# A fourth buffer for the raw weight tiles of a two-layer decoder, paid for with half the descriptor scratch of the software DMAs

## The chip, the cores and the metric

One core of a Trainium2 chip runs the whole program. The metric is the device time of one execution in microseconds (us). Before the change it is 982.41 us, the median of three runs (982.23 to 983.89 us).

## What is computed

The reference is a decoder trunk of two layers over 256 tokens of width 1024, in float32. Each layer is a half-step SwiGLU feed-forward network (FFN), a token-mixing block with three head groups, and a second half-step FFN, each followed by a layer norm of the scaled residual:

```python
def swiglu(x, wg, wu, wd):
    return (jax.nn.silu(x @ wg) * (x @ wu)) @ wd

for l in range(DEPTH):
    x = layer_norm(ALPHA * x + 0.5 * swiglu(x, ffn_wg[l, 0], ffn_wu[l, 0], ffn_wd[l, 0]), ln_g[l, 0], ln_b[l, 0])
    m = token_mix(x, w_in[l], w_out[l], ...)
    x = layer_norm(ALPHA * x + m, ln_g[l, 1], ln_b[l, 1])
    x = layer_norm(ALPHA * x + 0.5 * swiglu(x, ffn_wg[l, 1], ffn_wu[l, 1], ffn_wd[l, 1]), ln_g[l, 2], ln_b[l, 2])
```

`wg` and `wu` are 1024 x 2816, `wd` is 2816 x 1024, `w_in` is 1024 x 2344 and `w_out` is 1024 x 1024, so nearly all of the work is weights times activations, and every weight is read from memory once.

## The kernel before

The 256 tokens are two row tiles of 128 (t = 0 and 1). A float32 product is made of three passes of a faster format: both operands are split into a high part and a rest, and `mm3` (lines 262 to 264) issues high times high, high times rest and rest times high into one PSUM bank.

**How a weight reaches TensorE.** Weights come in "halves", tiles of 128 x 1024 floats (512 KB; 128 x 592 for one part of `w_in`). SyncE (SP) issues the load of a half into a tile `raw`. ScalarE (ACT) copies `raw` to `wh`, the high part (line 229 in `split_half`, line 217 in `split_tile`). VectorE (DVE) subtracts, `wl` = `raw` - `wh` (lines 230 and 218), and only then is the `raw` tile free for another load. `raw` has three buffers, `wh` and `wl` have eight each. Two halves are a unit, and `split_weights` makes units one to three ahead of their use. `PLAN`, a string of tokens, sets the order of the units in an FFN.

**Seven products.** For some pairs of weight chunks `seven` replaces eight block products by seven, over sums and differences of weight blocks that DVE builds (line 147). Its loads go to the tiles `fa`, `fb` and `fc`, and those of its function `f4` to two `raw` tiles (line 171, issued at line 143). Those two stay taken from their load until the product called "2", the last of a group, has had them split (line 218). The seven products are issued at line 415 into two PSUM banks. After product "3" DVE adds the bank to a copy (line 465), and product "2" overwrites that bank, so it waits for that add. Product "4", on the other bank, lies between.

**What follows.** Line 478 (ACT) and line 479 (DVE) gate the result into a tile `cc`, line 490 transposes it on TensorE, lines 267 and 268 split the transposed tile, and `down` multiplies by `wd`. The last three `down` units run for t = 0 and then for t = 1, and `layer_norm` (lines 349 to 360, one step of it on GpSimd at line 355) of t = 0 has the `down` work of t = 1 to hide behind. `make_xT` then transposes the normalised rows (line 290) for the next stage. In the mixing block ACT and DVE do, between the same weight splits, the gates (lines 584 to 631), keys and queries and the softmaxes.

**Order.** Inside an FFN the order of TensorE's instructions is pinned. On the other engines, and on TensorE elsewhere, a scheduler sets the order at build time from its own estimate of when buffers and results come free; each engine and each queue then runs its list strictly in order. A wait of ACT or DVE at the head of its list holds all that is behind it, and SP's loads stand in one list too.

**Software DMAs.** GpSimd issues 18 loads (layer norm parameters at line 337, small mixing weights of the second layer at line 535). The descriptors of such loads are written to a scratch area of every SBUF partition, whose size is `dynamic_dma_scratch_size`; a `raw` buffer takes 4096 bytes of a partition.

Of the kernel before, what the change touches and what calls it, by code (L numbers as in the profile page):

```python
# [18 lines left out]
F32 = mybir.dt.float32  # L19
# [38 lines left out]
def build(ctx, tc, d):  # L58
    nc = tc.nc
# [3 lines left out]
    wp = ctx.enter_context(tc.tile_pool(name="wp", bufs=1))  # L63
# [65 lines left out]
    def halves(src, w):  # L129
        units.append(lambda: [split_half(a, w) for a in src])  # L130

    def gate_up(l, f, c, q):
        return [d["wgu"][l, f, c, 2 * q + h] for h in range(2)]

    def seven(l, f, c):


        b11, b12, b21, b22 = [], [], [], []

        def load(to, src, pool, name, tags, bufs):  # L140
            for a, tag in zip(src, tags):
                to.append(pool.tile([128, 1024], F32, name=name, tag=tag, bufs=bufs))
                last_dma[0] = nc.sync.dma_start(out=to[-1], in_=a)

        def less(a, b, to):
            for x, y, z in zip(a, b, to):
                DVE.tensor_sub(out=z, in0=x, in1=y)  # L147

        def parts(ts):
            return [split_tile(x, 1024) for x in ts]  # L150

        def f1():
            load(b11, gate_up(l, f, c, 0), mix, "fa", ("qs0", "qs1"), 1)
            return parts(b11)

        def f5():
            load(b12, gate_up(l, f, c + 1, 0), wp, "fb", ("fb0", "fb1"), 1)
            less(b12, b11, b11)
            return parts(b11)

        def f6():
            load(b22, gate_up(l, f, c + 1, 1), mix, "fc", ("pT", "pT"), 3)
            less(b22, b11, b11)
            return parts(b11)

        def f7():
            less(b22, b12, b12)
            return parts(b12)

        def f4():  # L170
            load(b21, gate_up(l, f, c, 1), wp, "raw", ("raw", "raw"), 3)
            less(b21, b11, b11)
            return parts(b11)

        return {"1": f1, "5": f5, "6": f6, "7": f7, "3": lambda: parts(b22), "4": f4, "2": lambda: parts(b21)}

    for l in range(L):
# [34 lines left out]
    def split_tiles():  # L212
        return (wp.tile([128, 1024], F32R, name="wh", bufs=8), wp.tile([128, 1024], F32R, name="wl", bufs=8))

    def split_tile(raw, w):
        wh, wl = split_tiles()
        ACT.activation(out=wh[:, :w], in_=raw[:, :w], func=AF.Copy)  # L217
        DVE.tensor_sub(out=wl[:, :w], in0=raw[:, :w], in1=wh[:, :w].bitcast(F32))  # L218
        return wh, wl

    def split_half(src, w, parts=1, between=None):
        raw = wp.tile([128, 1024], F32, name="raw", bufs=3)
        wh, wl = split_tiles()
        for i in range(parts):
            s = slice(i * w // parts, (i + 1) * w // parts)
            last_dma[0] = nc.sync.dma_start(out=raw[:, s], in_=src[:, s])
            if between:
                between[i]()
            ACT.activation(out=wh[:, s], in_=raw[:, s], func=AF.Copy)  # L229
            DVE.tensor_sub(out=wl[:, s], in0=raw[:, s], in1=wh[:, s].bitcast(F32))  # L230
        return wh, wl
# [738 lines left out]
    def ffn(l, i, sums, after):  # L970

        f = Ffn(l, i, sums)
        if (l, i) == (0, 0):
            warm_up()
            load_x(0, 0)
            make_xT(0, (0,), sums)
            with tc.issue_after(last_pe[0].ins):
                warm_up()
            first = split_half(gate_up(0, 0, 0, 0)[0], 1024, 2, (lambda: load_x(0, 1), lambda: load_x(1, 0)))
            with tc.issue_after(last_pe[0].ins):  # L980
                make_xT(0, (1,), sums)
            load_x(1, 1)
            made.append([first, split_half(gate_up(0, 0, 0, 0)[1], 1024)])
            f.glu(0, 0, 0)
            with tc.issue_after(x1_after[0].ins):
                make_xT(1, sums=sums)
            f.glu(1, 0, 0)
            f.glu(0, 0, 1)
            f.glu(1, 0, 1)
            f.glu(0, 1, 0)  # L990
        else:
            f.glu(0, 0, 0)
            f.glu(0, 0, 1)
            f.glu(0, 1, 0)
            f.glu(1, 0, 0)
            f.glu(1, 0, 1)
# [118 lines left out]
```

## Time and profile before

| | |
|---|---|
| Median of 3 runs | 982.41 us |
| Profiled execution, its own time | 982.67 us |
| Its span, first to last instruction | 980.9 us |
| TensorE (PE) busy | 959.1 us, 98% of the span |
| DVE busy | 843.2 us, 86% |
| ACT busy | 583.1 us, 59% |
| GpSimd (POOL) busy | 34.8 us, 4% |
| Granted TensorE clock, mean | 0.997 of full speed |
| Read from memory | 176.91 MB, 181 GB/s over the span |
| Loads on the hardware queue | 171.23 MB, 52.8% of 16 DMA engines |
| Loads on the software queue | 6.75 MB, 2.3% |

The profiled execution is 0.26 us above the median. Its time outside the span is 982.67 - 980.9 = 1.8 us. The busy share of PE is a union over overlapping matmuls whose ends are modelled, so idle time of PE is time in which nothing at all was in flight there.

### The profile page before, as it was taken

How to read it: one execution, taken by the hardware profiler on the slowest of the kernel's cores; microseconds unless marked ns; L12 is line 12 of the kernel's file. 1: busy time of each engine (PE TensorE's matmuls, PEld its weight loads, DVE VectorE, ACT ScalarE, POOL GpSimd, SP SyncE). 2: the span in 40 equal slices, each digit the busy share in tenths (PEclk: the TensorE clock that was granted, in tenths of full speed). 3: DMA queues.
4: the chain of work that ended last, by engine and by line, in shares of the span. 5: the costliest groups of instructions: out<-in, count | busy, mean ns of one | idle time of the engine just before them, and what ended most of it. 6: DMA issues, size and time to landing. Idle time of an engine off the chain costs nothing. (4 is left out here: it accounts for less than half of the span.)

```text
span 980.9 us, 12843 instructions
## 1 busy us (share of the span) xinstructions
PE 959.1 (98%) x4611; PEld 780.5 (80%) x4611; DVE 843.2 (86%) x1247; ACT 583.1 (59%) x884; POOL 34.8 (4%) x50
## 2 busy tenths in 40 slices
PE   8999999999999999999999999999999999999996
PEld 5887888777778888888788888877787788888885
DVE  6798997887868988998899799978888699889986
ACT  6565664575764656565556666654667456556651
POOL 0000000020001000000000000001000010000000
PEclk9999999999999999999999999999999999999998
DMA  8765666564454645647673736466534364646251
GB/s 290 270 213 173 213 203 224 179 200 138 149 169 134 219 145 198 208 135 268 204 227 119 256 129 216 148 218 196 177 114 141 129 216 150 209 155 236 90 184 49
DMA packets 51872, 178.80 MB, mean 182 GB/s; under 512 B 6624, under 2 KB 7648, under 8 KB 51552
## 3 DMA queue, kind: packets, MB, share of 16 engines
q1 hardware_dynamic: 49968, 171.23, 52.8%
q0 software_dynamic: 1840, 6.75, 2.3%
q8 instruction: 36, 0.59, 0.2%
q14 instruction: 28, 0.23, 0.1%
HBM read 176.91 MB, written 1.05 MB: 181 GB/s over the span
## 5 line engine op out<-in xcount | busy, mean ns | idle before, releaser
L230 DVE TENSOR_TENSOR wl<-raw,wh 128x1024 fp32r<-128x1024 f32 (+2 forms) x225 | 267.7, 1202 | 60.5 <-ACT wh L229 59.8
L229 ACT ACTIVATE wh<-raw 128x1024 fp32r<-128x1024 f32 (+2 forms) x225 | 231.9, 1039 | 142.4 <-DMA raw<-in_wd 35.9
L217 ACT ACTIVATE wh<-fa 128x1024 fp32r<-128x1024 f32 x96 | 101.3, 1060 | 93.4 <-DVE fa L147 61.2
L262 PE MATMUL acc<-wh,hi 128*128 128x512 f32 x352 | 138.6, 394 | 0.0
L263 PE MATMUL acc<-wl,hi 128*128 128x512 f32 x352 | 137.2, 390 | 0.8 <-DVE wl L230 0.8
L264 PE MATMUL acc<-wh,lo 128*128 128x512 f32 x352 | 137.3, 390 | 0.0
L218 DVE TENSOR_TENSOR wl<-fa,wh 128x1024 fp32r<-128x1024 f32 x96 | 116.0, 1218 | 9.8 <-ACT wh L217 8.9
L263 PE MATMUL g<-wl,xh 128*128 128x512 f32 (+1 forms) x224 | 85.6, 382 | 1.6 <-DVE wl L230 1.6
L264 PE MATMUL g<-wh,xl 128*128 128x512 f32 (+1 forms) x224 | 86.3, 385 | 0.0
L262 PE MATMUL g<-wh,xh 128*128 128x512 f32 (+1 forms) x224 | 85.1, 381 | 0.0
L263 PEld LDWEIGHTS acc<-wl,hi 128*128 128x128 f32 x352 | 66.2, 188 | 14.5 <-DVE wl L230 1.1
L264 PEld LDWEIGHTS acc<-wh,lo 128*128 128x128 f32 x352 | 66.1, 188 | 13.9
L262 PEld LDWEIGHTS acc<-wh,hi 128*128 128x128 f32 x352 | 66.1, 188 | 13.8 <-ACT wh L229 0.4
L263 PE MATMUL acc<-wl,xh 128*128 128x512 f32 x128 | 51.5, 403 | 1.7 <-DVE wl L230 1.7
L262 PE MATMUL acc<-wh,xh 128*128 128x512 f32 x128 | 51.3, 402 | 1.1 <-ACT wh L229 1.1
L264 PE MATMUL acc<-wh,xl 128*128 128x512 f32 x128 | 50.5, 394 | 0.0
L262 PE MATMUL tr<-wh,xh 128*128 128x512 f32 x128 | 50.2, 392 | 0.0
L263 PEld LDWEIGHTS g<-wl,xh 128*128 128x128 f32 x224 | 42.1, 188 | 10.1 <-DVE wl L230 2.9
L264 PE MATMUL tr<-wh,xl 128*128 128x512 f32 x128 | 49.9, 390 | 0.0
L263 PE MATMUL tr<-wl,xh 128*128 128x512 f32 x128 | 49.8, 389 | 0.0
L262 PEld LDWEIGHTS g<-wh,xh 128*128 128x128 f32 x224 | 42.1, 188 | 8.2 <-issue 0.8
L264 PEld LDWEIGHTS g<-wh,xl 128*128 128x128 f32 x224 | 42.1, 188 | 6.9
(287 smaller groups left out, 1936.0 us busy)
## 6 DMA issues: line engine op xcount, KB each, us to landing
raw<-in_wgu SPq DMA_DIRECT2D x103, 512.0 KB, 4.1
raw<-in_wd SPq DMA_DIRECT2D x88, 512.0 KB, 4.5
raw<-in_win SPq DMA_DIRECT2D x32, 512.0 KB, 4.0
fa<-in_wgu SPq DMA_DIRECT2D x24, 512.0 KB, 4.1
fb<-in_wgu SPq DMA_DIRECT2D x24, 512.0 KB, 4.6
fc<-in_wgu SPq DMA_DIRECT2D x24, 512.0 KB, 4.8
raw<-in_wout SPq DMA_DIRECT2D x16, 512.0 KB, 3.8
lnp_ln_g<-in_ln_g POOLq DMA_DIRECT2D x5, 512.0 KB, 4.5
```

The source lines that it names most:

```text
L217: ACT.activation(out=wh[:, :w], in_=raw[:, :w], func=AF.Copy)
L218: DVE.tensor_sub(out=wl[:, :w], in0=raw[:, :w], in1=wh[:, :w].bitcast(F32))
L229: ACT.activation(out=wh[:, s], in_=raw[:, s], func=AF.Copy)
L230: DVE.tensor_sub(out=wl[:, s], in0=raw[:, s], in1=wh[:, s].bitcast(F32))
L262: pe(PE.matmul(ps, xh, wh, start=start, stop=False))
L263: pe(PE.matmul(ps, xh, wl, start=False, stop=False))
L264: pe(PE.matmul(ps, xl, wh, start=False, stop=stop))
```

## The change

The `raw` tiles get a fourth buffer, at both places that allocate them, and the scratch of the software DMAs goes from 8192 to 4096 bytes per partition.

```diff
         def f4():
-            load(b21, gate_up(l, f, c, 1), wp, "raw", ("raw", "raw"), 3)
+            load(b21, gate_up(l, f, c, 1), wp, "raw", ("raw", "raw"), 4)
...
     def split_half(src, w, parts=1, between=None):
-        raw = wp.tile([128, 1024], F32, name="raw", bufs=3)
+        raw = wp.tile([128, 1024], F32, name="raw", bufs=4)
...
-    nc = bacc.Bacc("TRN2", target_bir_lowering=False, num_devices=1, dynamic_dma_scratch_size=8192)
+    nc = bacc.Bacc("TRN2", target_bir_lowering=False, num_devices=1, dynamic_dma_scratch_size=4096)
```

No instruction is added or taken away. The scheduler, which knows of the fourth buffer, orders some instructions anew. POOL's list is the same, PE's differs at some 30 places outside the pinned stretches, and ACT's, DVE's and SP's lists differ at many.

SP, in the second FFN, around the two `raw` loads of `f4` (line 143); `in_wd` are weights of `down`:

```order
 L226 DMA raw<-in_wd 128x1024 x4
-L143 DMA raw<-in_wgu 128x1024
+L143 DMA raw<-in_wgu 128x1024 x2
 L143 DMA fb<-in_wgu 128x1024 x2
-L143 DMA raw<-in_wgu 128x1024
-L226 DMA raw<-in_wd 128x1024
+L226 DMA raw<-in_wd 128x1024 x2
 L143 DMA fc<-in_wgu 128x1024 x2
```

The two loads of `f4` stand together, and two loads of `down` weights instead of one stand ahead of the next `fc`.

DVE, in the last group of seven products of the same FFN, around the add after product "3" (line 465):

```order
 L479 SCALAR_TENSOR_TENSOR cc<-cc 128x256
 L218 TENSOR_TENSOR wl<-raw,wh 128x1024 x2
-L230 TENSOR_TENSOR wl<-raw,wh 128x1024
+L230 TENSOR_TENSOR wl<-raw,wh 128x1024 x2
 L465 TENSOR_TENSOR cc<-g_4000,cc 128x512
 L230 TENSOR_TENSOR wl<-raw,wh 128x1024
```

One more weight split stands ahead of the add. The same difference is in the last group of each of the four FFNs.

DVE, at the end of the same FFN, ahead of the layer norm of t = 0 (line 349):

```order
 L230 TENSOR_TENSOR wl<-raw,wh 128x1024
 L479 SCALAR_TENSOR_TENSOR cc<-cc 128x256
-L230 TENSOR_TENSOR wl<-raw,wh 128x1024 x2
+L230 TENSOR_TENSOR wl<-raw,wh 128x1024 x3
 L268 TENSOR_TENSOR lo<-tr_4357,hi 128x512
 L268 TENSOR_TENSOR lo<-tr_4366,hi 128x512
-L230 TENSOR_TENSOR wl<-raw,wh 128x1024 x3
+L230 TENSOR_TENSOR wl<-raw,wh 128x1024
 L349 SCALAR_TENSOR_TENSOR x_98<-x_98,acc_3457 128x512
```

One split moves ahead of the two rests of the transposed tile (line 268), and one leaves the stretch between them and the layer norm.

## Rows read from the trace of the kernel before

**Rows 1.** Stretches: busy us and count of PE, PEld, DVE, ACT, POOL; clock, DMA share, GB/s

```profile
0.00:25.00 25.00, 21.23 (x89) 14.40 (x90) 17.07 (x23) 15.34 (x22) 1.60 (x10) 1.00 0.84 291
...
75.00:250.00 175.00, 170.19 (x828) 138.68 (x827) 152.36 (x250) 104.95 (x177) 9.64 (x12) 1.00 0.58 188
...
475.00:500.00 25.00, 23.46 (x108) 19.06 (x107) 22.44 (x31) 13.58 (x17) 1.86 (x2) 1.00 0.65 202
500.00:650.00 150.00, 150.00 (x681) 123.75 (x680) 136.68 (x149) 93.28 (x118) 1.63 (x3) 1.00 0.54 181
650.00:725.00 75.00, 71.08 (x378) 58.66 (x377) 60.98 (x127) 41.15 (x80) 6.70 (x7) 1.00 0.53 174
...
950.00:980.90 30.90, 23.09 (x106) 18.85 (x104) 19.67 (x29) 5.52 (x7) 1.85 (x2) 0.91 0.25 87
```

**Rows 2.** Waits of PE: waiter <- releaser: us in total, times, longest us

```profile
PE acc L263 <- DVE wl L230: 2.5, 4, 1.0
PE tr L290 <- DVE x L360: 2.4, 2, 1.5
PE g L263 <- DVE wl L230: 1.6, 2, 0.8
PE acc L107 <- DVE zw L110: 1.2, 1, 1.2
PE tr L490 <- DVE cc L479: 1.2, 1, 1.2
PE acc L262 <- ACT wh L229: 1.1, 2, 0.7
PE tr L290 <- DMA x<-in_x: 1.0, 2, 0.7
PE tr L290 <- ACT c L584: 0.9, 1, 0.9
PE g L415 <- DVE cc L465: 0.8, 1, 0.8
PE tr L665 <- PE acc L281: 0.7, 2, 0.4
PE tr L290 <- DVE ksl L268: 0.5, 1, 0.5
```

**Rows 3.** Timeline of 478 to 490 us, end of the second FFN, all engines

```profile
479.77 4.04 SPq L226 DMA_DIRECT2D raw<-in_wgu  x3
...
481.13 1.06 ACT L229 ACTIVATE wh<-raw 128x1024 fp32r<-128x1024 f32 x1 [0.81 <-DMA raw<-in_wgu]
...
482.23 1.23 DVE L230 TENSOR_TENSOR wl<-raw,wh 128x1024 fp32r<-128x1024 f32 x1 [0.64 <-ACT wh L229]
483.37 0.68 DVE L349 SCALAR_TENSOR_TENSOR x<-x,acc 128x512 f32<-128x512 f32 x1
...
488.65 0.63 PE L290 MATMUL tr<-ident,x 128*128 128x128 f32 x4 [1.54 <-DVE x L360]
```

**Rows 4.** Instructions on tile raw: who waits on ACT's copy; landing of its loads

```profile
  ACT wh L229: 81.5, 67
...
DMA to landing us min/median/max: 2.7/4.2/8.1
```

**Rows 5.** Timeline of 459 to 468 us, last group of seven, second FFN

```profile
463.09 0.69 DVE L465 TENSOR_TENSOR cc<-g,cc 128x512 f32<-128x512 f32 x1 [1.06 <-PE g L415]
...
464.44 1.06 ACT L229 ACTIVATE wh<-raw 128x1024 fp32r<-128x1024 f32 x1 [4.40 <-DMA raw<-in_wd]
...
465.61 0.39 PE L415 MATMUL g<-wh,xh 128*128 128x512 f32 x1
```

**Rows 6.** Costliest groups: PE's first pass of `down`; busy us, mean ns of one

```profile
L262 PE MATMUL acc<-wh,hi 128*128 128x512 f32 x352 | 138.6, 394 | 0.0
```

**Rows 7.** GpSimd: its step of the layer norm, and its slowest kind of load

```profile
667.54 0.93 POOL L355 TENSOR_TENSOR ve<-ve,mhalf 128x1 f32<-128x1 f32 x1 [22.29 <-DVE ve L354]
...
lnp_ln_b<-in_ln_b POOLq DMA_DIRECT2D x5, 512.0 KB, 5.2
```

## The prediction

> **What bounds the kernel now.** I read the stretches first, because a busy share over the whole span hides where the idle time lies. PE is busy 150.00 of 150 us between 500 and 650 us: in the middle of an FFN it never stops, and nothing that comes earlier there can help [rows 1]. Its idle time lies in few places. It is 25.00 - 21.23 = 3.8 us in the first stretch (first loads), 4.8 us from 75 to 250, 1.5 us from 475 to 500, 3.9 us from 650 to 725 and 7.8 us at the end (the last layer norm and the store). The first and the last do not depend on a buffer that is reused, so what any change of the weight supply can win is in the middle: 4.8 + 1.5 + 3.9 = 10.2 us.
>
> The second view, who PE waited for, says what those 10.2 us are [rows 2]. The waits for `zw` and for `x` are the start, and so are one wait of 1.0 us for a rest `wl` and 0.4 us for a `wh`: 1.2 + 1.0 + 1.0 + 0.4 accounts for 3.6 of the first stretch's 3.8 us. The other waits are 1.5 (`wl` for `acc`), 0.7 (`wh`), 2.4 (layer norm, line 360), 1.6 (`wl` for `g`), 1.2 (line 490), 0.9 (line 584), 0.8 (line 465), 0.7 (line 665) and 0.5 us (`ksl`): 10.3 us.
>
> The third view, the timeline around one of them, shows why a layer norm is late [rows 3]. TensorE stood 1.54 us until 488.65. The norm of t = 0 began at 483.37, when DVE was done with a weight split that began at 482.23. That split had waited for ACT, and ACT had waited 0.81 us for a load to land; the next three `raw` loads left SP over 4.04 us, spread out because each needs a tile that DVE has freed. I followed the stops at 85, 181, 188, 227, 656, 680 and 707 us in the same way, and each led to a `raw` load that landed late: into a split that PE itself needs, or into a split that stood ahead of what PE needs on ACT or DVE.
>
> **What the fourth buffer does.** A load now waits for the split of the tile four before it, not three. A split takes DVE 1.23 us and ACT 1.06 us and a load takes 4.2 us to land (2.7 to 8.1) [rows 3, 4], so a tile is in use some 6.5 us, and three tiles give one half per 6.5 / 3 = 2.2 us, four one per 1.6 us. Where the supply is short, each load leaves one spacing, 1.6 to 2.2 us, earlier. No single stop is longer than 1.54 us, the one for line 360 [rows 2]. In the groups of seven the effect is larger: `f4` holds two tiles until product "2", which leaves the rest of the stream one tile of three now, and two of four after.
>
> The stops that lead to a late load, and go: 1.5 + 0.7 + 2.4 + 1.2 + 0.9 + 0.8 + 0.5 = 8.0 us in ten waits [rows 2]. Two kinds stay. The 1.6 us for `wl` into `g` stand behind DVE's own work of the gates: DVE had no idle time there. The 0.7 us at line 665 are PE after PE. A stop costs a little more than its idle time, because the last matmul before it is counted with its whole 394 ns [rows 6] although in the stream a matmul takes 150.00 / 681 = 0.22 us [rows 1]. That is an estimate of 0.17 us for each, 1.7 us for ten. Sum: 9.7 us.
>
> **What the change may take.** (a) Moved rows. The piece of DVE's order at line 465 puts a second split ahead of the add for which product "2" waits, at four places. The add ran at 463.09 and product "2" started at 465.61, so 465.61 - 463.09 - 0.69 = 1.8 us are to spare, and one split takes 1.23. Now that split's `raw` load landed just before 464.44, ACT having waited 4.40 us for it [rows 5]. If it stayed as late, the add would end at 464.44 + 1.06 + 1.23 + 0.69 = 467.4, 1.8 us after product "2" wants to start. I take it to be early, since its load no longer waits for a tile that `f4` holds. (b) At the layer norm of t = 0 the order has one split fewer ahead, which adds to the gain of rows 3; the two rests at line 268 get one more ahead. (c) In the mixing block some softmax and gate rows change places. The trace of before has no row for their new places. Bounds: below, nothing, or the 1.6 us of the two gate waits gained as well; above, as many new stops as there are old ones, 9.7 us, which undoes the sum. I take three new stops of the mean size of the ten, 3 x 0.8 = 2.4 us, since most of DVE's list is as it was. (d) The scratch. GpSimd issues few loads, far apart: it had waited 22.29 us in front of its step of the layer norm [rows 7]. So I take 0 for it; its upper end is the fourth rival.
>
> Sum: 9.7 - 2.4 = 7.3 us. The profiled execution is 982.67 us, 0.26 above the median, so the forecast is 982.41 - 7.3 = **975.1 us**. Its own range runs from three stops fewer gone to no new stop: 972.5 to 978.5.
>
> **Rivals.** *Loads only share the engines.* With three tiles in flight the DMA engines are already 0.65 busy at 202 GB/s around the stop of 488 us, and the first stretch, where all loads are free to go, reached no more than 291 GB/s at 0.84 [rows 1]. By that ceiling a half of 512 KB takes 1.8 us, and four tiles would give one per 1.8 us instead of 1.6. The trace speaks for some of it (landing times spread up to 8.1 us), and against all of it, since the share in the stretches with stops is 0.53 to 0.65. Half of the 9.7 us would go and the same share of new stops would come, 4.9 - 1.2 = 3.7: 978.7 us. The Trainium skill (DMA: Bandwidth & Descriptors, Issuing engines are not separate DMA queues) says that transfers issued at the same time run on the same 16 engines and interleave, which is this rival; its section Bandwidth puts what memory gives one core at about 358 GB/s, by which a half would take an estimated 1.46 us and this rival would be weak.
>
> *The wait moves.* The splits come earlier, but DVE, busy 136.68 of 150 us in the middle of an FFN [rows 1], or a `wh` buffer that TensorE still reads, ends last at the same places. For it: `wh` is not given a ninth buffer. Against it: of what waits on the `raw` tiles, 81.5 us are ACT's high parts waiting at 67 places [rows 4], and I found loads, not `wh`, at all stops that I count. The time would be within 0.2% of now, about 981.5.
>
> *The added split is late (slower).* The one mechanism is (a): on DVE, in the last group of each FFN, the split ahead of line 465. It decides if its load lands less than 1.8 us earlier than it does now (see (a)). If it lands no earlier at all, product "2" stops by 1.8 us at four places, 7.2 us, and with the layer norms behind it held as now (nothing gained), 982.4 + 7.2 = 989.6 us. Against it: at 464.44 the load had waited for a tile, which it now finds free.
>
> *The half scratch is too small (slower).* If descriptors of a load had to wait for the load before it to land, 5.2 us [rows 7], the next layer norm step on GpSimd could stand behind it. At the four norms with loads ahead of them in the list that would be up to 4 x 5.2 = 20.8 us, less the 7.3 gained: 996 us. The 22.29 us of slack speak against it [rows 7]. The Trainium skill (SBUF — State Buffer, SBUF size: 192, 224, or 256?) has 16 KiB set aside for this scratch as the normal case, four times what is left here; no run here shows the fill.
>
> **How the numbers follow.** Forecast 0.58, shared engines 0.20, the wait moves 0.11, added split 0.07, scratch 0.02, and 0.02 for more than the forecast's own range. A measurement of this kernel can tell some 0.2%, 2 us, from no change. Faster by more than that: 0.58 + 0.20 + 0.02 = 0.80. Within: 0.11. Slower: 0.09. The range leaves out at most 2 in 10: down to 9.7 + 1.6 = 11.3 us gained, 971.1, and up to the moved wait at 981.5.
>
> **What would show it.** Right: the waits of PE for lines 360, 479, 465 and 584 and for `acc`'s weights leave the list or fall under 0.3 us; PE is busy about 25.0 of 25 us around the second FFN's end; ACT's 81.5 us before its high parts from `raw` fall by a third or more. Shared engines: the median landing rises from 4.2 towards 5.6 us and the stops are halved. Added split: waits for line 465 four times. Scratch: POOL's step at line 355 waits for something other than DVE. Wrong altogether: PE's idle time between 25 and 950 us stays near 10 us.

## The result and the profile after

The changed kernel takes 978.29 us (median of 6 runs, 977.75 to 978.65), the kernel before 983.25 beside it (6 runs, 982.23 to 987.17): ratio 0.9938, 95% interval [0.9914, 0.9962]. That is 5.0 us faster by the medians; 7.3 were forecast, and 978.29 lies inside the range. The interval of the ratio means a gain of 3.7 to 8.5 us, so this measurement alone does not tell 5.0 from 7.3. The profiled executions are 982.67 us before (span 980.9) and 978.65 after (span 976.9).

The same stretches as in [rows 1], in the kernel after:

```profile
0.00:25.00 25.00, 20.94 (x87) 14.39 (x88) 17.16 (x23) 16.39 (x24) 1.60 (x10) 1.00 0.83 284
75.00:250.00 175.00, 172.91 (x845) 141.67 (x844) 154.24 (x254) 107.89 (x180) 9.59 (x12) 1.00 0.58 189
475.00:500.00 25.00, 24.50 (x113) 19.59 (x112) 21.99 (x33) 9.86 (x13) 2.52 (x4) 1.00 0.56 182
500.00:650.00 150.00, 149.98 (x677) 123.52 (x676) 138.28 (x148) 95.94 (x121) 0.97 (x2) 1.00 0.55 184
650.00:725.00 75.00, 72.72 (x393) 59.66 (x392) 60.62 (x148) 43.35 (x97) 6.66 (x7) 1.00 0.52 169
```

PE's idle time falls from 4.8 to 2.1 us between 75 and 250 us, from 1.5 to 0.5 around the second FFN's end, and from 3.9 to 2.3 between 650 and 725. The start is 0.3 us worse. What PE waited for, all of it, against [rows 2]:

```profile
PE acc L264 <- DVE lo L268: 2.0, 3, 0.8
PE g L263 <- DVE wl L230: 1.3, 2, 0.6
PE acc L107 <- DVE zw L110: 1.2, 1, 1.2
PE acc L290 <- DMA x<-in_x: 1.1, 1, 1.1
PE acc L263 <- DVE wl L230: 1.0, 1, 1.0
PE tr L290 <- ACT c L639: 0.8, 2, 0.4
PE tr L665 <- PE acc L281: 0.7, 2, 0.4
PE acc L262 <- ACT wh L229: 0.5, 1, 0.5
PE tr L290 <- DMA x<-in_x: 0.2, 1, 0.2
```

The waits for lines 360, 479, 465 and 584 and for `ksl` are gone. The 1.0 us for a `wl` and the 0.5 for a `wh` are the start's, so the weights of `acc` have no stop left inside. All ten stops that were to go went. Two kinds are new: 2.0 us for `lo`, the rests of the transposed tile (line 268), once at the end of each of the first three FFNs, and 0.8 us for `c` of line 639 in the mixing blocks. The gates' wait for `wl` is 1.3 us where it was 1.6.

The timeline at the end of the third FFN shows a new stop:

```profile
651.59 1.06 ACT L229 ACTIVATE wh<-raw 128x1024 fp32r<-128x1024 f32 x1 [2.68 <-DMA raw<-in_wd]
...
652.68 3.84 DVE L230 TENSOR_TENSOR wl<-raw,wh 128x1024 fp32r<-128x1024 f32 x4 [2.76 <-ACT wh L229]
...
654.96 1.06 ACT L267 ACTIVATE hi<-tr 128x512 fp32r<-128x512 f32 x2
...
655.93 0.40 PE L263 MATMUL acc<-wl,hi 128*128 128x512 f32 x1
656.43 1.28 DVE L268 TENSOR_TENSOR lo<-tr,hi 128x512 fp32r<-128x512 f32 x2
...
657.17 0.51 PE L264 MATMUL acc<-wh,lo 128*128 128x512 f32 x1 [0.84 <-DVE lo L268]
...
657.52 0.40 PE L262 MATMUL acc<-wh,hi 128*128 128x512 f32 x1
```

ACT waits 2.68 us for a load, and DVE 2.76 us for ACT; then DVE works through four splits in a row until 656.4. So the splits ahead of the rests are late ones, not early ones. The high parts `hi` stood at 654.96 + 1.06 = 656.0, the rests come behind the splits, and PE has caught up with them. From 655.93 to 657.52 PE starts two matmuls in 1.59 us, which take 0.23 us each in the stream: the stop of 0.84 us costs 1.13. At the layer norm of t = 0 in the second FFN, DVE now waits 2.30 us for PE, where before it was the splits that held it [rows 3].

On the tile `raw` the two lines of [rows 4] read after:

```profile
  ACT wh L229: 28.6, 32
...
DMA to landing us min/median/max: 2.8/4.3/9.2
```

The same view has what ACT and DVE stood idle for in front of their work on `raw`. Idle time until PE had done line 264 of `acc`, the last pass that reads a `wh`, was this before:

```profile
  PE acc L264: 31.4, 23
```

and this after:

```profile
  PE acc L264: 55.4, 45
```

With four `raw` tiles ACT waits less for loads and more for PE to release a `wh` buffer. PE loses nothing by it that its list of waits shows: of its waits for weights of `acc` only the start's are left.

### The profile page after: what moved, and what is told of

Read it like the earlier page. It is cut to its first block, busy times and chain, and to the rows that moved or that the text cites. A ratio compares the mean times of both kernels' runs of the same rounds, so it can differ in the third digit from the quotient of the medians.

```text
span 976.9 us, 12852 instructions
## 1 busy us (share of the span) xinstructions
PE 960.0 (98%) x4611; PEld 780.8 (80%) x4611; DVE 843.0 (86%) x1247; ACT 583.8 (60%) x884; POOL 34.7 (4%) x50
## 4 chain that ended last, share of the span: by engine, by line
PE 86%; DVE 6%; DMA 4%; ACT 2%; issue 2%; SPq 0%; DVEq 0%; ACTq 0%
PE g L415 12%; PE acc L264 11%; PE acc L262 11%; PE acc L263 11%; PE tr L415 8%; PE g L262 4%; PE g L263 4%; PE g L264 4%; PE tr L264 3%; PE tr L263 3%; PE tr L262 3%; DMA raw<-in_wd 3%; PE tr L290 3%; PE acc L281 2%; DVE wl L230 2%
## 5 line engine op out<-in xcount | busy, mean ns | idle before, releaser
L229 ACT ACTIVATE wh<-raw 128x1024 fp32r<-128x1024 f32 (+2 forms) x225 | 231.3, 1039 | 113.4 <-PE acc L264 55.4
```

## The experiments

Theory one: the buffer alone is worth some 9 to 10 us, as the sum had it, and the scheduler's new order of the rows takes about half of it back, mostly with the splits ahead of the rests at line 268. Rivals: the fourth buffer is worth no more than what was measured, because the loads share the engines; or the scratch costs something.

**The scratch alone.** Three buffers as before; the order of every engine is that of before.

```diff
-    nc = bacc.Bacc("TRN2", target_bir_lowering=False, num_devices=1, dynamic_dma_scratch_size=8192)
+    nc = bacc.Bacc("TRN2", target_bir_lowering=False, num_devices=1, dynamic_dma_scratch_size=4096)
```

> Three raw buffers as before, only the scratch of the software DMAs is halved; the order of every engine is that of before. My theory, that GpSimd has room to spare, expects no difference: within 0.1% of before (982.4 us, +-1), and no new wait of GpSimd's. The rival, that the smaller scratch costs something which the fourth buffer's gain hid, expects 1 to 3 us more than before.

Measured: 983.93 us (980.37 to 987.46, 10 runs) against 983.49; ratio 1.0003 [0.9985, 1.002]. GpSimd's step of the layer norm still waits for DVE alone, as in [rows 7]:

```profile
L355 POOL TENSOR_TENSOR ve<-ve,mhalf x12: 921/958/996, 185.0 to 974.8; 128x1 f32<-128x1 f32 x12
...
  DVE ve L354: 588.5, 10
```

The scratch has no price that this measurement can tell.

**The buffer alone, in the old order.** The changed kernel, with a table that holds the list of each engine in the order of the kernel before; it adds edges without a wait between neighbours of a list. A kernel pinned to its own order and otherwise unchanged was not run, so that the edges themselves cost nothing is taken and not shown.

```diff
             build(ctx, tc, d)
+            pin_order(tc)
...
+    for numbers in table.values():
+        names = [f"I-{n}" for n in numbers if f"I-{n}" in here]
+        for a, b in zip(names, names[1:]):
+            tc.add_manual_dep(here[b], a, info, reason="order")
```

> Four raw buffers and half the scratch, but every engine's list is pinned to the order that the kernel before had, so the buffer acts alone. Theory one, late loads: the stops of the kernel before end because the loads leave earlier, and the new stops of the changed kernel (2.0 us for the rests lo, 0.8 us for line 639) come from moved rows alone. Then PE's waits between 25 and 950 us fall from 10.3 to 2 to 3 us, with no wait for lo, and the time is 972 to 975 us, below the changed kernel's 978.3. Theory two, the new order did it: with the old order the late splits stand where they stood, and the time is 978.5 us or more.

Measured: 973.48 us (972.67 to 974.29, 4 runs), ratio 0.9891 [0.9876, 0.9906]. Its waits of PE:

```profile
PE g L263 <- DVE wl L230: 1.6, 2, 0.8
PE acc L290 <- DMA x<-in_x: 1.2, 1, 1.2
PE acc L107 <- DVE zw L110: 1.2, 1, 1.2
PE acc L263 <- DVE wl L230: 1.0, 1, 1.0
PE tr L665 <- PE acc L281: 0.7, 2, 0.4
PE acc L262 <- ACT wh L229: 0.4, 1, 0.4
PE tr L290 <- DMA x<-in_x: 0.2, 1, 0.2
```

Beyond the start only the two kinds are left that were to stay, 1.6 and 0.7 us. The gain is 983.49 - 973.48 = 10.0 us, twice that of the change as it stands, and the interval of the ratio lies wholly below the changed kernel's. At the third FFN's end the rests stand behind two splits and not four:

```profile
648.47 2.47 DVE L230 TENSOR_TENSOR wl<-raw,wh 128x1024 fp32r<-128x1024 f32 x2 [3.12 <-ACT wh L229]
650.86 1.28 DVE L268 TENSOR_TENSOR lo<-tr,hi 128x512 fp32r<-128x512 f32 x2
```

**The rests first.** The changed kernel in its own order, pinned in the same way, with only the pair of high parts (ACT) and the pair of rests (DVE) of the last transposed tile moved ahead in the first three FFNs. DVE in the second FFN, the changed kernel (-) and this one (+):

```
-L230 TENSOR_TENSOR wl<-raw,wh 128x1024 x3
+L230 TENSOR_TENSOR wl<-raw,wh 128x1024 x2
 L268 TENSOR_TENSOR lo<-tr_4357,hi 128x512
 L268 TENSOR_TENSOR lo<-tr_4366,hi 128x512
-L230 TENSOR_TENSOR wl<-raw,wh 128x1024
+L230 TENSOR_TENSOR wl<-raw,wh 128x1024 x2
```

> The changed kernel with its own order pinned, except that at the end of the first three FFNs the high parts and rests of the last transposed tile stand one or two weight splits earlier in ACT's and DVE's lists. Theory, moved rows: PE's 2.0 us in three waits for lo (line 268) vanish with their refills, 2.0 + 3 x 0.17 = 2.5 us: 975.8 us beside the changed kernel's 978.3. Rival, the splits that move behind become what PE waits for (line 263 for acc): 977.5 to 978.5 us.

Measured: 975.11 us (975.04 to 975.6, 4 runs), ratio 0.9909 [0.9894, 0.9924]. Of PE's waits the one for `lo` is gone and the ones in the mixing blocks are there still:

```profile
PE g L263 <- DVE wl L230: 1.3, 2, 0.6
...
PE tr L290 <- ACT c L639: 0.8, 2, 0.4
```

So three pairs of moved rows are worth 978.29 - 975.11 = 3.2 us by these medians, and 977.65 - 975.11 = 2.5 us by the changed kernel's second measurement (below): between half and two thirds of what the order costs.

**Two buffers.** The dose in the other direction, with the scheduler's own order for two, so that count and order change together.

```diff
-            load(b21, gate_up(l, f, c, 1), wp, "raw", ("raw", "raw"), 4)
+            load(b21, gate_up(l, f, c, 1), wp, "raw", ("raw", "raw"), 2)
...
-        raw = wp.tile([128, 1024], F32, name="raw", bufs=4)
+        raw = wp.tile([128, 1024], F32, name="raw", bufs=2)
```

> Two raw buffers, half the scratch, order by the scheduler. By the spacing of the prediction two tiles give one half per 6.5 / 2 = 3.25 us, more than the 2.7 us that 12 matmuls on one half take, and the two loads of f4 take both tiles at once. Theory: PE stops in every FFN, ACT's wait for loads is several times the 81.5 us of before, and the time is 1040 to 1120 us. Rival, loads only share the DMA engines, so that the count of tiles in flight matters little: under 1000 us.

Measured: 1036.23 us in a single execution, 52.7 above the 983.49 of three buffers and a little under the expected range. What waits on the loads grows, to 2.2 times the value of before and not to several times:

```profile
  ACT wh L229: 175.9, 115
...
DMA to landing us min/median/max: 2.7/3.8/8.8
```

ACT's high parts wait 175.9 us with two tiles, 81.5 with three [rows 4], 25.8 with four in the old order. The median landing time moves little with it (3.8, 4.2 and 4.3 us), so by the median more loads in flight slow each other by half a microsecond at most.

**The mixing blocks in the old order, and both pieces.** Two kernels more, pinned in the same way: the changed kernel's order with the rows of ACT, DVE and PE inside the two mixing blocks taken from the kernel before (the three counts in the text below are in this order of the engines), and the same with the rests first. A piece of ACT's list in the first mixing block, the changed kernel (-) and this one (+):

```
 L639 ACTIVATE c_1869<-acc_1820 128x512
+L642 ACTIVATE kv_1871<-acc_1820 128x256
+L229 ACTIVATE wh<-raw 128x1024
 L627 ACTIVATE eb_1813<-bc_1808 128x128
 L628 ACTIVATE enb_1814<-bc_1808 128x128
 L631 ACTIVATE ekh_1815<-bc_1808,bl_1811 128x64 x2
-L229 ACTIVATE wh<-raw 128x1024 x2
-L642 ACTIVATE kv_1871<-acc_1820 128x256
+L229 ACTIVATE wh<-raw 128x1024
```

> The changed kernel, with the rows of PE, ACT and DVE inside the two mixing blocks put back to the order of the kernel before (92, 134 and 276 rows lie in the stretches that differ); the feed-forward blocks and SP's loads keep the new order. Theory: the cost of the new order is local, and what is left of it beside the rests at line 268 sits in the mixing blocks (two stops of 0.4 us for c of line 639, and about 0.5 us twice in the attention between line 665 and line 895). From the traces of the run with the rests first and of the run with the whole old order (975.1 against 973.5 us) this part is 1.6 us, by their spans 2.4: 976.4 us, 975.9 to 976.9, with the stops at line 268 (2.0 us) still there and the stops for c of line 639 gone. Rival: the rest of the cost comes from SP's new order of the loads, which stays: then 978.3 us as the changed kernel.

> Both local repairs in one kernel: the rests at the ends of the first three feed-forward blocks ahead, and the mixing blocks in the order of before; SP's loads and the rest of the feed-forward rows stay in the new order. Theory: the two pieces add up and are the whole cost of the new order: 973.5 us as the run with the whole old order (973.0 to 974.2). Rival: SP's new order of the loads has a price of its own: 975 us, no better than with the rests alone.

> The changed kernel itself, unedited, beside the two others on one chip: 978.3 us (977.7 to 978.7). Were it at 976 or less here, the differences between this day's runs and its own earlier time would be the chip's and not the order's.

Measured on one chip (before 984.46 us there, 981.13 to 986.56, 11 runs):

| kernel | us, median (lowest to highest) | ratio to before |
|---|---|---|
| the changed kernel again | 977.65 (976.54 to 978.75) | 0.9936 [0.9919, 0.9953] |
| mixing blocks in the old order | 975.83 (974.38 to 979.48) | 0.9921 [0.9901, 0.9942] |
| both pieces | 973.78 (972.69 to 976.4) | 0.9901 [0.9881, 0.992] |

The changed kernel repeats its time. By the medians the mixing blocks give 1.8 us and the rests 2.1 on top. The intervals of one piece overlap with the changed kernel's, and the traces don't give the two sizes either. In the profiled execution with the mixing blocks in the old order the stops for `c` of line 639 are gone, as expected, but the stops for `lo`, expected at 2.0 us, are nearly gone as well, though their rows stand in the new order:

```profile
PE acc L264 <- DVE lo L268: 0.2, 1, 0.2
```

The same execution has a fall of TensorE's clock that cost it up to 1.7 us (last section). What is shown is the two pieces together, 977.65 - 973.78 = 3.9 us: every run with both is faster than every run of the changed kernel (976.4 is under 976.54), though only just, and their intervals touch. With both, PE's list of waits has neither `lo` nor line 639.

With both pieces the kernel is within 0.3 us of the whole old order by the medians, and within 1.0 by the ratios to the kernel before, since the two were measured on two chips. A price of SP's new order of the loads, or of the feed-forward rows that stay new, of that size would not show.

In the profile of the changed kernel run again, the wait for `lo` is smaller than in the first, at a span of 974.8:

```profile
PE tr L290 <- ACT c L639: 0.9, 2, 0.4
...
PE acc L264 <- DVE lo L268: 0.5, 2, 0.4
```

So what the rests cost in the new order differs from execution to execution: 0.2, 0.5 and 2.0 us of idle time in three profiles. What decides it was not tried.

## Why the prediction was right, and where not

**Late loads held PE: right.** Ten stops were to go, 8.0 us of idle time and 1.7 for the refill after them, 9.7 us. With the buffer alone in the old order all ten are gone and 10.0 us are gained. The refill was put at 0.17 us for each; the one stop read above shows 0.29.

**Two kinds stay: right.** The gates' 1.6 us are 1.3 after and 1.6 in the old order; line 665 keeps its 0.7.

**The moved rows: the term that was mis-sized.** The prediction took "three new stops of the mean size of the ten, 3 x 0.8 = 2.4 us". The order costs 978.29 - 973.48 = 4.8 us, or 977.65 - 973.78 = 3.9 by the other comparison. In the profiled execution the idle time comes out near it, 2.0 + 0.8 - 0.3 = 2.5 us, but that is partly luck: the count of three had no row behind it, the stops are five, at places that it had not priced, and in the second profile of the same kernel they come to 0.5 + 0.9 - 0.3 = 1.1 us. Two things were left out. First, the new stops need a refill as the old ones did: five stops at the 0.29 us of the one read above are an estimated 1.4 us. Second, PE's own list differs in the mixing blocks, and work in another order can take longer without a stop. Eight products of `pT` and `vbd` (line 281, 64 columns of weights) run as two, a pair of transposes, and six in the changed kernel:

```profile
252.24 0.65 PE L281 MATMUL acc<-pT,vbd 128*64 128x256 f32 x2
252.81 0.44 PE L290 MATMUL tr<-ident,c 128*128 128x128 f32 x2
253.18 1.08 PE L281 MATMUL acc<-pT,vbd 128*64 128x256 f32 x6
```

and in a row with the buffer alone in the old order:

```profile
250.13 1.08 PE L281 MATMUL acc<-pT,vbd 128*64 128x256 f32 x8
```

The eight take no longer than the six: by their records in the trace they start two at a time, 0.01 us apart, while the first two and the last two of the changed kernel start one by one. That is 0.65 + 1.08 - 1.08 = 0.65 us, and the second mixing block has the same rows, so 1.3 us. Both kernels with the mixing blocks in the old order have the eight in a row again; this piece alone was not tried. 2.5 + 1.4 + 1.3 = 5.2 us, between the 4.8 of the medians and the 976.9 - 970.9 = 6.0 of the two profiled executions from which the terms are read. The prediction also named the place of the largest new stop, in (b), "the two rests at line 268 get one more ahead", and gave it no price of its own. One split is 1.23 us of DVE [rows 3], more than the 0.84 us that the longest of these stops lasts, so it was worth following in the timeline as line 465 was. The inner range does not follow from its terms: no new stop gives 982.41 - 9.7 = 972.7 and not 972.5, and three stops fewer gone, 3 x 0.97 = 2.9 us, give 978.0 and not 978.5.

**The added split at line 465: no stop**, as forecast. PE's list of waits has no line 465 any more.

**The scratch: 0**, as taken, and now with an interval.

**Loads only share the engines: fell as the main limit, and its ceiling was too low.** The time that this rival gave, 978.7 us, is nearer to the result than the forecast is, but for another reason: the median landing went from 4.2 to 4.3 us and not towards 5.6, no old stop was halved, and the buffer alone gives the whole gain. Its 291 GB/s were a mean over a stretch with engines at 0.83 to 0.84. Where the engines are full, in the kernel after from 168 to 170 us, the row of the stretches reads:

```profile
168.00:170.00 2.00, 2.00 (x11) 1.65 (x9) 0.00 (x0) 0.19 (x1) 0.00 (x0) 1.00 1.02 414
```

and ACT, which waits for each load there, begins its high parts 1.22 to 1.27 us apart:

```profile
169.81 1.06 ACT L229 ACTIVATE wh<-raw 128x1024 fp32r<-128x1024 f32 x1 [2.33 <-DMA raw<-in_wd]
171.08 1.06 ACT L229 ACTIVATE wh<-raw 128x1024 fp32r<-128x1024 f32 x1 [0.20 <-DMA raw<-in_wd]
172.34 1.06 ACT L229 ACTIVATE wh<-raw 128x1024 fp32r<-128x1024 f32 x1 [0.20 <-DMA raw<-in_wd]
173.56 1.06 ACT L229 ACTIVATE wh<-raw 128x1024 fp32r<-128x1024 f32 x1 [0.17 <-DMA raw<-in_wd]
```

So a half can land every 1.27 us here, at 414 GB/s. The Trainium skill (DMA: Bandwidth & Descriptors, Bandwidth) has about 358 GB/s as one core's share of memory, by which a half was put at an estimated 1.46 us. The same section has 425 GB/s measured in transfers of 16 MB with the other core of the pair idle. One core runs here, and the trace is nearer to that figure.

In one respect the rival holds. These four are the splits that stand ahead of the rests at the end of the first FFN, and the first of the new stops, 0.65 us at 176.54, comes behind them, so there the shared engines do make the splits late. In the old order the engines are as full at that place:

```profile
166.00:168.00 2.00, 2.00 (x11) 1.65 (x10) 1.12 (x2) 0.98 (x2) 0.00 (x0) 1.00 1.02 406
```

and PE has no stop behind it. Full engines alone don't stop PE; the order adds what is missing.

**The wait moves: in part, by another way.** ACT's 81.5 us fell to 28.6, well over the third that was asked for, and PE between 475 and 500 us is busy 24.50 of 25, not 25.0: the 0.5 us are the rests. Part of ACT's wait did move to the `wh` buffers, as this rival had it (31.4 to 55.4 us), but PE shows no stop by it. What PE waits for moved to the list of DVE, where splits whose loads land late stand ahead of what PE needs next.

**The best version** is the fourth buffer in the old order, 973.48 us, ratio 0.9891 to the kernel before.

## What to carry to other kernels

A changed buffer count also changes the order that a scheduler finds, and the two have to be costed apart: pin the old order once, and the gain of the buffer and the price of the order can be read one by one. With one buffer more the scheduler put one weight split more ahead of work that was due, so follow what stands behind the supply in the lists of the engines that prepare the operands; one row more ahead of an operand needs the same price as a wait. A new stop costs its idle time and the refill after it, as an old one does. And small matmuls that run two at a time lose that when the order separates them, without a stop to show for it.

## What the runs showed of the hardware that was not expected

With two buffers TensorE's granted clock is below full in stretches where PE stops often. The rows are 0 to 25, 75 to 250 and 650 to 725 us; the column before the DMA share is the clock:

```profile
0.00:25.00 25.00, 19.25 (x76) 12.85 (x77) 14.53 (x20) 12.91 (x19) 1.60 (x10) 0.93 0.77 268
75.00:250.00 175.00, 163.93 (x733) 130.49 (x732) 139.29 (x172) 97.34 (x137) 8.52 (x9) 0.97 0.56 186
650.00:725.00 75.00, 67.36 (x300) 53.39 (x298) 56.46 (x71) 33.89 (x45) 3.16 (x4) 0.95 0.43 144
```

PE is busy 67.36 of 75 us in the last, and the kernel before had 71.08 there at 1.00 [rows 1]. PE's busy time over the whole span is 981.1 us with two buffers and 960.0 in the changed kernel, for the same 4611 matmuls: some 21 us that are not idle time. By the clock column these three stretches lose at most 25 x 0.07 + 175 x 0.03 + 75 x 0.05 = 10.8 us of them; a matmul before a stop is also counted longer than one in the stream, and how much of the rest that is was not read.

In the profile of the kernel with the mixing blocks in the old order the clock fell once more, between 228 and 232 us:

```profile
220.00:228.00 8.00, 7.62 (x48) 6.41 (x47) 6.76 (x19) 3.54 (x11) 0.55 (x1) 1.00 0.57 214
228.00:232.00 4.00, 4.00 (x23) 3.95 (x23) 2.12 (x12) 0.23 (x1) 0.00 (x0) 0.57 0.00 0
232.00:240.00 8.00, 8.00 (x43) 6.67 (x41) 6.57 (x26) 5.11 (x11) 1.09 (x2) 1.00 0.34 83
```

A mean of 0.57 says that the clock stood at the lower of its two levels, 1.2 and not 2.4 GHz, for most of these 4 us, which costs at most 4.00 x 0.43 = 1.7 us. PE had been busy 7.62 of the 8 us ahead of it, in the last 2.6 of them with the small matmuls of line 665. With both pieces the same stretch holds 27 matmuls in place of 23 at a clock of 1.00:

```profile
228.00:232.00 4.00, 4.00 (x27) 3.37 (x26) 3.21 (x21) 0.94 (x2) 0.00 (x0) 1.00 0.00 0
```

Why it fell in the one execution and not in the other stays open.
